# Four modulation groups change place: two from matmuls to multiply-and-sum in the mixer, two from the mixer into the feed-forward

## The chip, the cores and the metric

The kernel runs on one core of one Trainium2 chip. The metric is the time of one execution on the device in microseconds (us), lower is better. Engines are named TensorE (PE in the profile; its weight loads are PEld), VectorE (DVE), ScalarE (ACT), GpSimd (POOL) and SyncE (SP, which here only issues DMAs).

## The reference, cut to what matters

A two-layer encoder over two sequences of 256 and 512 tokens, 1024 wide, float32. Each layer is modulated by a conditioning vector c: a matrix product of silu(c) with a 1024 x 6144 matrix gives six vectors of 1024, for the shift, the scale and the gate of the layer's two halves.

```python
def trunk(x, c, adaln_w, adaln_b, norm_g, ...):
    for l in range(DEPTH):                       # 2 layers
        mod = jax.nn.silu(c) @ adaln_w[l] + adaln_b[l]
        sh1, sc1, g1, sh2, sc2, g2 = [t[:, None, :] for t in jnp.split(mod, 6, axis=-1)]
        h = rmsnorm(x, norm_g[l, 0]) * (1 + sc1) + sh1
        y = mlstm_mixer(h, ...) if l == 0 else swa_mixer(h, ...)
        x = x + g1 * y
        h = rmsnorm(x, norm_g[l, 1]) * (1 + sc2) + sh2
        x = x + g2 * conv_ffn(h, ...)
    return rmsnorm(x, final_g)

def conv_ffn(h, w_up, conv_w, conv_b, w_down):
    u = conv1d(h @ w_up, conv_w, width=3) + conv_b       # 2 * 2816 channels
    return (silu(u[..., :D_FF]) * u[..., D_FF:]) @ w_down
```

The six vectors are called modulation groups 0 to 5 here. Both sequences (c has two rows) go through the same trunk.

## The kernel before, in words

All 768 tokens are kept transposed, channels on the 128 partitions. Every float32 operand of a large product is split into a high part (`hi`, rounded by a ScalarE copy) and a low part (`lo`, a VectorE subtraction), and a product is three matmuls: hi x hi, hi x lo, lo x hi (`fp_copy_split`, lines 271 to 279; `mm`, line 268). A weight is loaded by SP into one of five `raw` slots of 512 KB (`raw`, line 282), split into one of three `whi`/`wlo` pairs, and its slot is free when the subtraction has read it. All operations of the split have the lines 275 and 276 in the profile, and all ordinary matmuls line 269.

Larger things live in six slots called `slab`, 12 KB a partition, which are handed out by order of allocation and come free when the last instruction on the old content is done. In a feed-forward they hold: x (two), `urows` (two, the second in use to the end), and of each part p `yrow` (the convolved rows) and `g` (the gated product, split).

The order of instructions on each engine is planned at build time from an estimate of costs (`schedule_with_timeline_sim=True`), earlier lines of the program before later ones where both are ready; stretches under `manual_schedule` keep the written order on the engines named. On the chip every engine runs its list in order and waits by semaphores.

The modulation. Layer 0's groups 0 and 1 come first (`adaln`). Its groups 2 to 5 are computed inside the mLSTM mixer on TensorE by `adaln_g`: eight loads of 512 KB of `adaln_w`, 32 matmuls of 256 columns against `silc` (silu(c), 32 columns wide, four side by side), two copies, two transposes and the sums with the bias. Layer 1's 48 columns of 128 (six groups of eight) are computed inside the same mixer on VectorE by `adaln_v`: of each column, 128 rows of the transposed matrix (`adaln_t`, 512 KB) are loaded into a `raw` slot, and for each sequence s one instruction multiplies them with silu(c), laid out along every partition (`row`), and sums along the row (`tensor_tensor_reduce`, line 538 in the profile, with the read of the sum behind it). A column is loaded one step before it is used.

Both are generators, and the mixer calls them step by step: `self.step(self.fill)` for the columns and `self.step(self.fillp)` for the matmul groups stand between its projections, its value tiles and its chunks, in heads 1 to 3; in the output gates behind the heads (line 892) only `fill` is stepped. What is left runs at the mixer's end (line 1742).

The feed-forward (`ffn`) has 11 parts of 256 gate and 256 value channels. Part p: `up(p)` computes two pairs of 128-channel rows with a seven-product scheme (`pair`; GpSimd makes the sums of weight quarters, lines 1383 to 1395; the matmuls have lines 1350, 1351 and 1353), convolves them (`conv`, lines 1587, 1589, 1590), applies silu (line 1597, held back into the next pair), multiplies on GpSimd and splits into `g` (`product`, lines 1602 and 1603). `down(p - 1)`, the product of the previous part with its share of `w_down`, comes behind `up(p)`, and adds its result to x with the gate (`resid`, line 602).

Of the kernel before, what the change touches and what calls it, by code (L numbers as in the profile page):

```python
# [11 lines left out]
F32 = mybir.dt.float32  # L12
R = mybir.dt.float32r
# [168 lines left out]
class Net:  # L182
# [335 lines left out]
                    self.cst(NG + (2 * l + i) * 8, 8), ALU.add, ALU.mult,  # L518
                )

    def adaln_v(self, l, pool):

        nc = self.nc
        stt = nc.vector.scalar_tensor_tensor
        row = pool.tile([P, 2, 1024], F32, name="crow")
        nc.sync.dma_start(row, self.crow.to_broadcast([P, 2, 1024]))
        junk = pool.tile([P, 1024], F32, name="junk")
        mod = self.mod[l]
        fetch = lambda j: self.raw(self.io["adaln_t"][j])
        nxt = fetch(0)  # L530
        yield
        for j in range(48):
            w, nxt = nxt, fetch(j + 1) if j < 47 else None
            with ExitStack() as order:
                if j == 0:
                    order.enter_context(self.tc.issue_after(self.opened.ins))
                for s in range(2):
                    nc.vector.tensor_tensor_reduce(  # L538
                        out=junk, in0=w, in1=row[:, s], scale=1.0, scalar=self.cst(AB + 48 * l + j),
                        op0=ALU.mult, op1=ALU.add, accum_out=mod[:, j, s : s + 1],  # L540
                    )
            i = {15: 0, 39: 1}.get(j)
            if i is not None:
                for s in range(2):
                    stt(
                        self.gain[l][i][:, :, s], mod[:, j - 7 : j + 1, s], 1.0,
                        self.cst(NG + (2 * l + i) * 8, 8), ALU.add, ALU.mult,
                    )
            yield
# [105 lines left out]
    def product(self, o, w, act, c0, c1, ks):  # L655
        wh, wl = (t.rearrange("p (k m) -> p k m", k=KC) for t in w)
        for k in ks:
            ah, al = act(k, c0, c1)
            self.mm(o, wh[:, k], ah, k == 0, False)
            self.mm(o, wh[:, k], al, False, False)  # L660
            self.mm(o, wl[:, k], ah, False, k == KC - 1)
# [910 lines left out]
    def ffn(self, l, xt, pool, last_tile, apply, keep=None):  # L1572
# [22 lines left out]
        def silu(yrow):  # L1595
            for j in range(2):
                nc.scalar.activation(yrow[:, j], yrow[:, j], AF.Silu)

        def product(yrow, g):
            for j in range(2):  # L1600
                y = yrow[:, 2 + j]
                nc.gpsimd.tensor_tensor(y, y, yrow[:, j], ALU.mult)  # L1602
                self.fp_copy_split(g[:, 0, j], g[:, 1, j], y)

        def up(p):
            urow = urows[0] if p == 0 else urows[1]
            fixed = lambda i: self.bank[i][:, :H]
            if p == 0:
                eng = mybir.EngineType
                self.ready(HALVES[0])  # L1610
                with self.tc.manual_schedule(engines={eng.PE, eng.Activation, eng.DVE}):
                    behind[:] = self.head(u0, last_tile, pool, urows, mark, early)
            yrow = self.slab([P, 4, TG])
            g = self.slab([P, 2, 2, TG], R)
            for i in range(2):
                if p:
                    rows = [urow[:, 2 * i + j] for j in range(2)]
                    with ExitStack() as order:
                        for ins in behind[2 * i :] if p == 1 else ():
                            order.enter_context(self.tc.issue_after(ins))  # L1620

                        other = p == i == 1
                        bank = lambda j: self.pa()[:, :H] if j == 1 and other else fixed(j)
                        self.pair(pool, u0 + 3 * p + i, bank, rows, p == 1, held.pop() if held else None)
                for j in range(2):
                    conv(urow[:, 2 * i + j], yrow[:, 2 * i + j], i * FC + 2 * p + j)
                if i == 0:
                    held.append(lambda: silu(yrow))
            if p:
                product(yrow, g)  # L1630
            else:
                gate = held.pop()
                held.append(lambda: (gate(), product(yrow, g)))
            return g

        def mark(t):

# [45 lines left out]

        prev = None
        for p in range(NPART):
            g = up(p)
            if prev is not None:
                down(*prev)
            prev = (p, g)
        down(*prev)  # L1690


# [27 lines left out]
    def first(self, pool):  # L1720
# [15 lines left out]
            self.nc.gpsimd.memset(t.bitcast(F32), 0.0)  # L1736
        hi, lo = (t.rearrange("p (j m) -> p j m", m=32)[:, :, 0:4] for t in gates)
        self.fp_copy_split(hi, lo, narrow.rearrange("p (j m) -> p j m", m=4))
        self.fillp = chain(*(self.adaln_g(0, grp) for grp in range(2, 6)))
        self.fill = self.adaln_v(1, pool)  # L1740
        act = self.mlstm(pool, gates, xt)
        for _ in chain(self.fillp, self.fill):
            pass
# [53 lines left out]
def _pack(inp):  # L1797
# [42 lines left out]
            w[u + 2] = _unit_D(inp["ffn_w_down"][l][p * 256 : (p + 1) * 256])  # L1840
    arr["w"] = w
    arr["adaln_w"] = np.ascontiguousarray(inp["adaln_w"][:1])
    arr["adaln_t"] = np.ascontiguousarray(inp["adaln_w"][1].T).reshape(48, P, D)
    arr["crow"] = np.ascontiguousarray(c.T.reshape(16, P))
    arr["rel_bias"] = np.ascontiguousarray(inp["rel_bias"])
    return arr
# [25 lines left out]
```

## Time and profile before

| what | value |
|---|---|
| time, median of 3 runs | 1808.51 us (1806.85 to 1808.69) |
| the profiled execution's own time | 1808.25 us, span 1806.4 us |
| granted TensorE clock, mean | 0.996 |
| busy: PE / PEld / DVE / ACT / POOL | 1773.1 / 1644.4 / 1384.8 / 887.8 / 488.2 us |
| HBM traffic | 176.77 MB read, 6.44 MB written, 101 GB/s over the span |

The stages lie, by the trace, so: the opening to about 65 us, the mLSTM mixer to about 425 us (its output gates from 353 us), its output projection and the first feed-forward to about 1000 us, the attention mixer, its projection and the second feed-forward to the end. Busy time of an engine counts its instructions' time on the engine alone; matmuls overlap, so that of PE is a union. A wait in the trace names the instruction that waited and the one that ended its wait.

### The profile page before, as it was taken

To read this page: it belongs to the slowest core of one execution; us is meant where nothing else is said; L and a number is where in the kernel's file an instruction comes from. 1 tells how busy PE (TensorE), PEld (TensorE's weight loads), DVE (VectorE), ACT (ScalarE), POOL (GpSimd) and SP (SyncE) were. 2 spreads that over 40 slices of the span, in tenths; PEclk is the share of its full clock that TensorE was granted. 3 is DMA by queue.
4 is the path that set the end of the run, shared out by engine and by line. 5 is a ranking of instruction groups with operands and counts; after the bars stand their busy time and mean duration, and the time that the engine had idled before them with its cause. 6 is when DMAs were issued, how large, how long until landed. Compare 5 with 4: busy or idle time off the path is not lost.

```text
span 1806.4 us, 28907 instructions
## 1 busy us (share of the span) xinstructions
PE 1773.1 (98%) x11206; PEld 1644.4 (91%) x11206; DVE 1384.8 (77%) x2219; ACT 887.8 (49%) x1789; POOL 488.2 (27%) x397
## 2 busy tenths in 40 slices
PE   7999999999999999999999999999999999999998
PEld 4988888889998999999999999889989999999997
DVE  4876777895799778777777867767998777777877
ACT  4544433444565444444444657665564444444443
POOL 3000000031024333333331313320144333333323
PEclk9999999999999999999999999999999999999999
DMA  9344665656212222222223331234122222222212
GB/s 360 98 140 135 196 207 180 215 180 219 71 59 71 62 67 71 70 71 71 67 64 94 106 93 42 60 92 138 48 82 71 71 71 71 70 70 71 70 36 71
DMA packets 64997, 185.08 MB, mean 102 GB/s; under 512 B 6247, under 2 KB 24839, under 8 KB 64732
## 3 DMA queue, kind: packets, MB, share of 16 engines
q1 hardware_dynamic: 64284, 182.72, 31.3%
q8 instruction: 88, 1.44, 0.3%
q10 hardware_dynamic: 576, 0.52, 0.1%
q14 instruction: 49, 0.40, 0.1%
HBM read 176.77 MB, written 6.44 MB: 101 GB/s over the span
## 4 chain that ended last, share of the span: by engine, by line
PE 87%; DVE 5%; DMA 3%; ACT 3%; issue 1%; POOL 1%; SPq 0%; DVEq 0%; ACTq 0%; POOLq 0%
PE ps L269 28%; PE pa L269 24%; PE ps L1350 11%; PE ps L1351 10%; PE ps L1353 10%; DMA raw<-in_adaln_t_dram 1%; PE pa L1189 1%; DVE junk L538 1%; DMA slab<-in_adaln_w_dram 1%; DVE wlo L276 1%; PE pa L1350 0%; PE pa L1351 0%; PE pa L1353 0%; ACT zh L1301 0%; DMA raw<-in_adaln_w_dram 0%
## 5 line engine op out<-in xcount | busy, mean ns | idle before, releaser
L275 ACT CAST whi<-raw 128x1024 fp32r<-128x1024 f32 (+1 forms) x231 | 241.0, 1045 | 339.0 <-PE pa L269 144.4
L276 DVE TENSOR_TENSOR wlo<-raw,whi 128x1024 fp32r<-128x1024 f32 (+1 forms) x231 | 312.6, 1354 | 119.1 <-ACT whi L275 116.8
L269 PE MATMUL pa<-slab,whi 128*128 128x256 f32 (+1 forms) x1280 | 307.6, 335 | 0.0
L269 PEld LDWEIGHTS pa<-slab,whi 128*128 128x128 f32 x1280 | 222.2, 188 | 21.6 <-DVE slab L602 0.4
L602 DVE SCALAR_TENSOR_TENSOR slab<-pa,mod,slab 128x256 f32<-128x256 f32 (+1 forms) x320 | 187.2, 603 | 62.7 <-PE pa L269 62.6
L269 PE MATMUL pa<-slab,wlo 128*128 128x512 f32 (+1 forms) x640 | 205.7, 334 | 0.0
L269 PE MATMUL ps<-zh,whi 128*128 128x256 f32 (+1 forms) x560 | 188.1, 337 | 0.3 <-ACT zh L948 0.3
L269 PE MATMUL ps<-zl,whi 128*128 128x256 f32 (+1 forms) x560 | 183.6, 330 | 0.5 <-DVE zl L563 0.5
L269 PE MATMUL ps<-zh,wlo 128*128 128x256 f32 (+1 forms) x560 | 181.7, 330 | 0.0
L1350 PE MATMUL ps<-zh,whi 128*128 128x384 f32 x504 | 172.6, 342 | 3.8 <-ACT nt L1421 2.0
L269 PE MATMUL ps<-slab,whi 128*128 128x384 f32 (+2 forms) x704 | 172.0, 329 | 0.9 <-DVE slab L276 0.5
L1351 PE MATMUL ps<-zl,whi 128*128 128x384 f32 x504 | 169.9, 337 | 0.8 <-DVE zl L1307 0.8
L1353 PE MATMUL ps<-zh,wlo 128*128 128x384 f32 x504 | 169.1, 336 | 0.0
L538 DVE CUSTOM_DVE_ANT_0 junk<-raw,crow,cstt 128x1024 f32<-128x1024 f32 x96 | 125.2, 1305 | 25.1 <-DMA raw<-in_adaln_t_dram 24.5
L1386 POOL TENSOR_TENSOR raw<-raw,raw 128x512 f32<-128x512 f32 x40 | 53.8, 1344 | 319.4 <-DVE wlo L276 246.3
L269 PEld LDWEIGHTS pa<-slab,wlo 128*128 128x128 f32 x640 | 120.4, 188 | 13.2 <-DVE wlo L276 0.4
L1602 POOL TENSOR_TENSOR slab<-slab 128x772 f32<-128x772 f32 x44 | 86.5, 1969 | 163.7 <-DVE slab L1590 150.5
L1589 DVE SCALAR_TENSOR_TENSOR slab<-slab,cstt,slab 128x771 f32<-128x771 f32 x88 | 105.4, 1200 | 26.5 <-ACT slab L1587 26.4
L269 PEld LDWEIGHTS ps<-slab,whi 128*128 128x128 f32 x704 | 122.5, 188 | 3.4 <-ACT whi L275 0.9
L269 PEld LDWEIGHTS ps<-zh,whi 128*128 128x128 f32 x560 | 106.8, 191 | 12.8 <-issue 3.5
L269 PEld LDWEIGHTS ps<-zl,whi 128*128 128x128 f32 x560 | 106.8, 191 | 9.5 <-DVE zl L563 0.7
L269 PE MATMUL ps<-slab,wlo 128*128 128x384 f32 (+2 forms) x352 | 114.8, 328 | 0.1
(301 smaller groups left out, 4286.8 us busy)
## 6 DMA issues: line engine op xcount, KB each, us to landing
raw<-in_w_dram SPq DMA_DIRECT2D x208, 512.0 KB, 3.7
raw<-in_adaln_t_dram SPq DMA_DIRECT2D x48, 512.0 KB, 4.2
raw<-in_adaln_w_dram SPq DMA_DIRECT2D x36, 512.0 KB, 4.5
slab<-in_x_dram SPq DMA_DIRECT2D x12, 512.0 KB, 7.2
slab<-in_adaln_w_dram SPq DMA_DIRECT2D x11, 512.0 KB, 9.2
slab<-mrows SPq DMA_DIRECT2D x8, 384.0 KB, 6.3
xs<-slab SPq DMA_DIRECT2D x6, 512.0 KB, 3.6
bt<-brow SPq DMA_DIRECT2D x16, 192.0 KB, 3.1
```

The source lines that it names most:

```text
L269: self.nc.tensor.matmul(out, lhsT, rhs, start=start, stop=stop)
L275: nc.scalar.copy(hi, src)
L276: return nc.vector.tensor_tensor(lo, src, hi.bitcast(F32), ALU.subtract)
L538: nc.vector.tensor_tensor_reduce(out=junk, in0=w, in1=row[:, s], scale=1.0, scalar=self.cst(AB + 48 * l + j), op0=ALU.mult, op1=ALU.add, a ...
L602: return self.nc.vector.scalar_tensor_tensor(x, o, self.mod[l][:, gc + c, q : q + 1], x, ALU.mult, ALU.add)
L1189: nc.tensor.transpose(pp[:, ks], b.t[:, e, ks], self.ident)
L1350: mm(o, wh[:, k], hi[k], start=start and k == 0, stop=False, skip_group_check=True)
L1351: mm(o, wh[:, k], lo[k], start=False, stop=False, skip_group_check=True)
L1353: mm(o, wl[:, k], hi[k], start=False, stop=k == 3, skip_group_check=True)
L1386: tt(q[0], q[2], q[0], ALU.subtract)
L1589: stt(y[:, 1:], u[:, :-1], w(0), y[:, 1:], ALU.mult, ALU.add)
L1602: nc.gpsimd.tensor_tensor(y, y, yrow[:, j], ALU.mult)
```

## The change

Layer 0's groups 4 and 5 are no longer computed by `adaln_g`; `fillp` holds groups 2 and 3 alone. `adaln_v` becomes `by_rows(columns, room)`, which takes any list of columns of both layers (0 to 47 layer 0, 48 to 95 layer 1) and the room for `row` and its scratch. In the mixer it runs over layer 1's groups 0 and 1 (48 to 63), layer 0's groups 4 and 5 (32 to 47) and layer 1's groups 2 and 3 (64 to 79): 48 columns, as before. Layer 1's groups 4 and 5 (80 to 95) run inside the first layer's feed-forward: at part 2 a third slab is taken for `row` (1 MB) and scratch, and each pair (two to a part) from part 2 on makes one step. To free that slab `g` is allocated later: `product` now only multiplies, and the splits (`parted`) with their allocation of `g` come behind `down(p - 1)` in parts 1 to 10, in both layers. The transposed matrix in memory holds both layers.

```diff
--- before.py
+++ after.py
@@ -518,21 +518,21 @@
                     self.cst(NG + (2 * l + i) * 8, 8), ALU.add, ALU.mult,
                 )
 
-    def adaln_v(self, l, pool):
+    def by_rows(self, columns, room):
 
         nc = self.nc
         stt = nc.vector.scalar_tensor_tensor
-        row = pool.tile([P, 2, 1024], F32, name="crow")
+        row, junk = room[:, :2], room[:, 2]
         nc.sync.dma_start(row, self.crow.to_broadcast([P, 2, 1024]))
-        junk = pool.tile([P, 1024], F32, name="junk")
-        mod = self.mod[l]
-        fetch = lambda j: self.raw(self.io["adaln_t"][j])
+        fetch = lambda i: self.raw(self.io["adaln_t"][columns[i]])
         nxt = fetch(0)
         yield
-        for j in range(48):
-            w, nxt = nxt, fetch(j + 1) if j < 47 else None
+        for i, at in enumerate(columns):
+            w, nxt = nxt, fetch(i + 1) if i + 1 < len(columns) else None
+            l, j = divmod(at, 48)
+            mod = self.mod[l]
             with ExitStack() as order:
-                if j == 0:
+                if i == 0:
                     order.enter_context(self.tc.issue_after(self.opened.ins))
                 for s in range(2):
                     nc.vector.tensor_tensor_reduce(
@@ -1596,11 +1596,15 @@
             for j in range(2):
                 nc.scalar.activation(yrow[:, j], yrow[:, j], AF.Silu)
 
-        def product(yrow, g):
+        def product(yrow):
             for j in range(2):
                 y = yrow[:, 2 + j]
                 nc.gpsimd.tensor_tensor(y, y, yrow[:, j], ALU.mult)
-                self.fp_copy_split(g[:, 0, j], g[:, 1, j], y)
+
+        def parted(yrow, g):
+            for j in range(2):
+                self.fp_copy_split(g[:, 0, j], g[:, 1, j], yrow[:, 2 + j])
+            return g
 
         def up(p):
             urow = urows[0] if p == 0 else urows[1]
@@ -1611,7 +1615,9 @@
                 with self.tc.manual_schedule(engines={eng.PE, eng.Activation, eng.DVE}):
                     behind[:] = self.head(u0, last_tile, pool, urows, mark, early)
             yrow = self.slab([P, 4, TG])
-            g = self.slab([P, 2, 2, TG], R)
+            if p == 2 and l == 0:
+                self.fill = self.by_rows(range(80, 96), self.slab([P, 3, 1024]))
+                self.step(self.fill)
             for i in range(2):
                 if p:
                     rows = [urow[:, 2 * i + j] for j in range(2)]
@@ -1626,12 +1632,15 @@
                     conv(urow[:, 2 * i + j], yrow[:, 2 * i + j], i * FC + 2 * p + j)
                 if i == 0:
                     held.append(lambda: silu(yrow))
+                if p > 1:
+                    self.step(self.fill)
             if p:
-                product(yrow, g)
-            else:
-                gate = held.pop()
-                held.append(lambda: (gate(), product(yrow, g)))
-            return g
+                product(yrow)
+                return lambda: parted(yrow, self.slab([P, 2, 2, TG], R))
+            g = self.slab([P, 2, 2, TG], R)
+            gate = held.pop()
+            held.append(lambda: (gate(), product(yrow), parted(yrow, g)))
+            return lambda: g
 
         def mark(t):
 
@@ -1683,10 +1692,10 @@
 
         prev = None
         for p in range(NPART):
-            g = up(p)
+            part = up(p)
             if prev is not None:
                 down(*prev)
-            prev = (p, g)
+            prev = p, part()
         down(*prev)
 
 
@@ -1736,8 +1745,8 @@
             self.nc.gpsimd.memset(t.bitcast(F32), 0.0)
         hi, lo = (t.rearrange("p (j m) -> p j m", m=32)[:, :, 0:4] for t in gates)
         self.fp_copy_split(hi, lo, narrow.rearrange("p (j m) -> p j m", m=4))
-        self.fillp = chain(*(self.adaln_g(0, grp) for grp in range(2, 6)))
-        self.fill = self.adaln_v(1, pool)
+        self.fillp = chain(*(self.adaln_g(0, grp) for grp in range(2, 4)))
+        self.fill = self.by_rows([*range(48, 64), *range(32, 48), *range(64, 80)], pool.tile([P, 3, 1024], F32, name="crow"))
         act = self.mlstm(pool, gates, xt)
         for _ in chain(self.fillp, self.fill):
             pass
@@ -1840,7 +1849,7 @@
             w[u + 2] = _unit_D(inp["ffn_w_down"][l][p * 256 : (p + 1) * 256])
     arr["w"] = w
     arr["adaln_w"] = np.ascontiguousarray(inp["adaln_w"][:1])
-    arr["adaln_t"] = np.ascontiguousarray(inp["adaln_w"][1].T).reshape(48, P, D)
+    arr["adaln_t"] = np.ascontiguousarray(inp["adaln_w"].transpose(0, 2, 1)).reshape(96, P, D)
     arr["crow"] = np.ascontiguousarray(c.T.reshape(16, P))
     arr["rel_bias"] = np.ascontiguousarray(inp["rel_bias"])
     return arr
```

## The prediction

> **What bounds the kernel now.** I read the page's first and fourth parts, then the waits of TensorE by stage, then the stages' windows.
>
> ```profile
> PE 1773.1 (98%) x11206; PEld 1644.4 (91%) x11206; DVE 1384.8 (77%) x2219; ACT 887.8 (49%) x1789; POOL 488.2 (27%) x397
> PE 87%; DVE 5%; DMA 3%; ACT 3%; issue 1%; POOL 1%; SPq 0%; DVEq 0%; ACTq 0%; POOLq 0%
> ```
>
> TensorE is busy nearly throughout and carries the chain that ended last; the reader should still ask whether that holds in the two stages that change. The waits of TensorE, first for 130 to 430 us (the mixer), then for 600 to 980 us (the first layer's feed-forward), answer it with one line each:
>
> ```profile
> PE pa L738 <- ACT slab L734: 0.4, 1, 0.4
> PE ps L1350 <- ACT ps L1410: 0.2, 1, 0.2
> ```
>
> So in both stages TensorE waits for practically nothing: its issued work is the time there. The windows of four stretches (columns: busy time of PE, its weight loads, DVE, ACT, POOL; granted clock; DMA share; GB/s) tell how near the others are:
>
> ```profile
> 260.00:310.00 50.00, 49.63 (x340) 41.01 (x339) 32.01 (x70) 16.57 (x48) 3.64 (x2) 1.00 0.59 198
> 310.00:353.00 43.00, 43.00 (x324) 36.27 (x323) 33.79 (x72) 17.04 (x40) 0.00 (x0) 1.00 0.63 205
> 353.00:420.00 67.00, 67.00 (x407) 60.02 (x406) 59.45 (x96) 29.73 (x64) 23.51 (x16) 1.00 0.63 202
> 700.00:800.00 100.00, 100.00 (x569) 94.23 (x568) 77.34 (x87) 46.07 (x73) 39.84 (x24) 1.00 0.22 68
> ```
>
> The clock is 1.00 in all four, so it plays no part. VectorE is next: 71% of 260 to 353 us, 89% of 353 to 420 us, 77% in the feed-forward.
>
> **The change part by part.**
>
> *Two groups leave TensorE.* Modulation groups 4 and 5 of layer 0 are no longer matmuls against silc. The matmuls that read silc, all four groups, in the mixer's first and second half, and the transposes that end a group:
>
> ```profile
> L269 PE MATMUL ps<-raw,silc 128*32 128x256 f32 x256 | 22.0, 386 | 0.0
> 130.00:195.00 65.00, 5.96 (x80) 2.19 (x80) 0.00 (x0) 0.00 (x0) 1.00 0.46 148
> 195.00:260.00 65.00, 3.83 (x48) 1.37 (x48) 0.00 (x0) 0.00 (x0) 1.00 0.58 190
> 260.00:353.00 93.00, 12.24 (x128) 4.05 (x128) 0.00 (x0) 0.00 (x0) 1.00 0.61 201
> L507 PE MATMUL ps<-kct,sb x8: 271/272/273, 190.5 to 352.6; 128*128 128x128 f32 x8
> ```
>
> A group has 64 records. The first two groups took 5.96 + 3.83 = 9.8 us, the last two, which go, 12.2 us; the last two are cut into smaller bursts, and each burst's last matmul overlaps what follows it. Half of all four is 11.0 us, and I take that; ends 9.8 and 12.2. Four transposes of 0.27 us go too; they overlap their neighbours, and I count 0.3 us. Gain on TensorE 11.3 us.
>
> *What those bursts covered.* Some stand directly before work that was only just ready. TensorE's timeline at the end of head 3:
>
> ```profile
> 342.02 0.63 PE L269 MATMUL ps<-raw,silc 128*32 128x256 f32 x6
> 342.58 2.17 PE L269 MATMUL pa<-slab,PT 128*128 128x258 f32 x16
> 344.69 0.63 PE L269 MATMUL ps<-raw,silc 128*32 128x256 f32 x4
> 345.25 1.46 PE L269 MATMUL pa<-slab,PT 128*128 128x258 f32 x10
> 346.63 1.06 PE L269 MATMUL ps<-raw,silc 128*32 128x256 f32 x12
> 347.62 0.74 PE L269 MATMUL pa<-slab,PT 128*128 128x258 f32 x4
> ```
>
> From start to start the six cost 342.58 - 342.02 = 0.56 us and the twelve 0.99 us: they do hold TensorE's queue. If the PT products were not ready earlier, TensorE would idle there instead. The one wait of the mixer, 0.4 us for L734, stands behind such a burst. The order of the matmuls is planned anew at each build and the next head's projections are independent, so most of this refills. I charge 1.3 us (the 0.4 us grown by one burst of 0.9 to 1.0); ends 0 and 5.6, half the gain.
>
> *The mixer's column work on VectorE keeps its count.* 48 columns before, 48 after (16, 16 and 16), at the same steps, in the same room; only their order and source differ. Two groups' copies and sums leave VectorE (some 1 us). SP issues 16 fewer loads of adaln_w there. Where a load now is late, VectorE waits at a column:
>
> ```profile
> L538 DVE CUSTOM_DVE_ANT_0 junk<-raw,crow,cstt 128x1024 f32<-128x1024 f32 x96 | 125.2, 1305 | 25.1 <-DMA raw<-in_adaln_t_dram 24.5
> L538 DVE DVE_READ_ACCUMULATOR2_ANT mod<- 128x1 f32 x96 | 7.8, 81 | 0.0
> ```
>
> With fewer loads competing for the five raw slots that wait can only shrink; I count nothing. With 11.3 us less of TensorE, VectorE's share of 260 to 353 us goes from 65.8 of 93 to about 65 of 82 (79%), below the 89% of the next stretch, where TensorE never waited.
>
> *Sixteen columns enter the first layer's feed-forward.* Parts 2 to 9 get two columns each: 2 x 2 x (1.305 + 0.081) = 5.5 us of VectorE per part. A part's length is the distance between two first products on GpSimd:
>
> ```profile
> 700.59 1.87 POOL L1602 TENSOR_TENSOR slab<-slab 128x772 f32<-128x772 f32 x1 [5.40 <-DVE slab L1590]
> 747.04 1.87 POOL L1602 TENSOR_TENSOR slab<-slab 128x772 f32<-128x772 f32 x1 [5.40 <-DVE slab L1590]
> ```
>
> That is 46.45 us. VectorE's 77% of it is 35.9 us, with the columns 41.4 us or 89%. That is the share of 353 to 420 us, where 26 column instructions, POOL work at 35% and a full TensorE lived side by side. This row is the nearest and it says: no cost. But GpSimd slows VectorE:
>
> ```profile
> 740.35 1.29 POOL L1383 TENSOR_TENSOR raw<-raw 128x512 f32<-128x512 f32 x1 [7.23 <-DMA raw<-in_w_dram]
> 740.45 2.27 DVE L276 TENSOR_TENSOR wlo<-raw,whi 128x1024 fp32r<-128x1024 f32 x1 [2.06 <-ACT whi L275]
> 743.58 1.21 DVE L276 TENSOR_TENSOR wlo<-raw,whi 128x1024 fp32r<-128x1024 f32 x1
> ```
>
> The same split took 1.21 us alone and 2.27 us when it began just after a GpSimd sum. The Trainium skill ("SBUF — State Buffer", section "Who interferes with whom") gives a rule for it: a VectorE instruction with two SBUF inputs and a GpSimd one that reads SBUF exclude each other for a whole instruction, in order of issue. The pair above agrees, 1.06 us lost to a sum with 1.19 us left. By the rule, with POOL at 40%, about 13 of the 32 instructions would be held by up to a sum's length, at 1.06 us each some 14 us more on VectorE, 93% of a part rather than 89%. On TensorE that costs only what is not covered. I charge 1.5 us for all parts; ends 0 and 32 x 1.06 = 34 us.
>
> *The loads.* Sixteen loads and the 1 MB broadcast row join SP's queue of weight loads, which always waits for a slot. What SP waited for over the span, what GpSimd waited for in the feed-forward, and the load:
>
> ```profile
> SPq L284 <- DVE wlo L276: 1098.6, 167, 20.6
> POOL raw L1386 <- DVE wlo L276: 121.8, 16, 14.2
> POOL raw L1383 <- DMA raw<-in_w_dram: 66.6, 15, 8.8
> raw<-in_adaln_t_dram SPq DMA_DIRECT2D x48, 512.0 KB, 4.2
> ```
>
> A column holds a slot for its landing (4.2 us) and its two instructions (2.7 us), 6.9 us, or 13.8 us a part of the 5 x 46.45 = 232 us of slots: weight loads come 13.8 / 5 = 2.8 us later. The next user, the sums of L1383, precedes L1386, and L1386 stands idle 121.8 / 16 = 7.6 us waiting for a split, not for the load: 2.8 us is hidden. The row is fetched once, in part 2, into a slab that is free only when part 1's splits are done; queued behind it on SP are part 2's weights, and the first column. A part is 46 us; I count nothing.
>
> *The splits of g move behind the down-projection before them.* In layer 0 with the extra slab two slabs are left for yrow and g, so g(p) waits for the last matmul of part p-1's down-projection, and the next yrow for those splits:
>
> ```profile
> L276 DVE TENSOR_TENSOR slab<-slab,slab 128x772 fp32r<-128x772 f32 x44 | 53.1, 1208 | 0.0
> L275 ACT CAST slab<-slab 128x772 fp32r<-128x772 f32 x44 | 36.8, 836 | 26.6 <-POOL slab L1602 26.2
> 721.88 0.49 DVE L602 SCALAR_TENSOR_TENSOR slab<-pa,mod,slab 128x256 f32<-128x256 f32 x1 [0.92 <-PE pa L269]
> 726.65 1.04 ACT L1587 ACTIVATE slab<-slab,cstt 128x772 f32<-128x772 f32 x1 [1.88 <-DVE slab L1423]
> ```
>
> Two casts and two subtractions, 0.84 + 2 x 1.21 = 3.3 us in a pipeline, fit between that part's last residual (721.9 us) and the next part's first convolution (726.7 us); behind other splits on VectorE they may run 2 us late, but their reader is the next down-projection, over 20 us on. The last part of each layer has no next up-projection between: its splits stand behind at most the sixteen residuals, two subtractions at 1.21 us, 2.4 us a layer if they came last. They are ready in the middle of that down-projection and go when ready: 0; end 4.8.
>
> **Sum.** -11.0 - 0.3 + 1.3 + 1.5 = -8.5 us on TensorE's path. The profiled execution took 1808.25 us (span 1806.4), 0.26 below the runs' median of 1808.51, so the two can be used alike. 1808.25 - 8.5 = 1799.75, say 1799.8 us.
>
> **The rivals.**
>
> *The cover is lost.* The bursts filled waits, and half of their time stays as idle before L738, L720 and the PT products. For it: the 0.4 us at L734. Against: the stretch without bursts, 353 to 420 us, has none. 1808.25 - 5.65 + 1.5 = 1804.1 us. [...]
>
> *VectorE comes late in the feed-forward (slower).* A column stands before a split or an eviction that TensorE needs. For it: in both feed-forwards one such wait exists, in part 1:
>
> ```profile
> PE ps L1353 <- DVE s1l L276: 2.8, 2, 1.4
> ```
>
> At 1.4 us for each of 16 steps it is 22.4 us: 1808.25 - 11.3 + 1.3 + 22.4 = 1820.7. It decides from (10.0 + 3.6) / 8 = 1.7 us a part. Against: that row is two waits in 1806 us, and 353 to 420 us has 89% without any.
>
> *The slots bind.* If the 2.8 us of later weights showed in each of 8 parts: 22.4 us, the same time, told apart by who is waited for (ACT whi behind DMA). Half hidden, it gives 1809.5, no change. Against: L1386's idle time.
>
> **How the numbers follow.** About 0.2% (3.6 us) is what a measurement tells from no change. My forecast with its own range, 1796 to 1803: 0.62, all faster. The cover lost: 0.18, of it 0.12 faster, 0.06 same, as it ends at the border. VectorE late: 0.13, of it 0.08 slower, 0.05 same where it is partial. Slots: 0.07, of it 0.01 faster, 0.03 same, 0.03 slower. Faster 0.75, same 0.14, slower 0.11. The range goes from 1796 (11.3 + 1.2 for the longer bursts, no cost) to 1807, which leaves out the worse half of the last three cases.
>
> **What would show it.** Right: 128 silc matmuls instead of 256 in the mixer, TensorE full from 260 us on, the out-projection starting some 10 us earlier; 32 column instructions in parts 2 to 9 of the first feed-forward, 1.3 to 2.3 us long; a part still 46.4 to 46.7 us. Wrong: parts 2 to 9 above 48 us, with TensorE waiting for DVE s1l, wlo or L1423; TensorE waiting for ACT L734 or the PT casts after 260 us; new waits at the layers' last down-projection.

## The result, and the profile after

The changed kernel takes 1815.53 us (median of six runs, 1812.78 to 1817.0) beside 1808.06 us for the kernel before on the same chip (six runs, 1806.8 to 1808.78): a ratio of 1.0040, 95% interval 1.0027 to 1.0053. It is slower by 7.5 us; 1799.8 was predicted, in a range of 1796 to 1807. Times here and below are medians of fast runs; one slow run, 5135.94 us of the last kernel in the table, is left out.

The page of the changed kernel, first and fourth part: TensorE has shed 6.6 us of busy time, VectorE has taken on 40.9 us, and the chain leans on VectorE more than before (7% instead of 5%).

```profile
PE 1766.5 (97%) x11074; PEld 1642.4 (91%) x11074; DVE 1425.7 (79%) x2277; ACT 889.0 (49%) x1787; POOL 488.1 (27%) x397
PE 82%; DVE 7%; DMA 4%; issue 3%; ACT 2%; POOL 2%; SPq 0%; DVEq 0%; POOLq 0%; ACTq 0%
```

First products on GpSimd mark the parts. Of the kernel before: parts 0, 2 and 8.

```profile
539.18 2.51 POOL L1602 TENSOR_TENSOR slab<-slab 128x772 f32<-128x772 f32 x1 [5.97 <-ACT slab L1597]
607.37 1.86 POOL L1602 TENSOR_TENSOR slab<-slab 128x772 f32<-128x772 f32 x1 [6.79 <-DVE slab L1590]
885.80 1.89 POOL L1602 TENSOR_TENSOR slab<-slab 128x772 f32<-128x772 f32 x1 [3.92 <-DVE slab L1590]
```

The same three of the changed kernel:

```profile
522.81 2.51 POOL L1602 TENSOR_TENSOR slab<-slab 128x772 f32<-128x772 f32 x1 [5.97 <-ACT slab L1597]
606.21 1.85 POOL L1602 TENSOR_TENSOR slab<-slab 128x772 f32<-128x772 f32 x1 [5.10 <-DVE slab L1590]
893.69 1.86 POOL L1602 TENSOR_TENSOR slab<-slab 128x772 f32<-128x772 f32 x1 [0.96 <-DVE slab L1590]
```

The mixer gained 539.18 - 522.81 = 16.4 us. From part 0 to 2 the lead shrinks to 1.2 us: 83.4 us instead of 68.2, a loss of 15.2. From part 2 to 8 another 9.1 goes: 287.5 instead of 278.4, 1.5 a part. The marks are GpSimd's, and TensorE's work between them is not quite the same, as the windows from part 0 to 2 show, of before and of the change:

```profile
539.18:607.37 68.19, 65.12 (x366) 61.18 (x365) 59.58 (x61) 36.60 (x57) 27.43 (x15) 1.00 0.26 81
522.81:606.21 83.40, 73.62 (x389) 68.27 (x388) 71.65 (x80) 38.97 (x61) 29.71 (x15) 0.96 0.35 108
```

The change has 23 matmuls more there and 18 fewer from part 2 to 8 (1569 instead of 1587). At 278.43 / 1587 = 0.175 us each, some 4 us of the 15.2 are work that has moved ahead of the mark and some 3 us must be added to the 9.1: as losses they are rather 11 and 12 us. After the last columns nothing more is lost, and the second layer's feed-forward, with the later splits alone, keeps its parts of some 46.4 us.

What TensorE waited for from 525 to 1010 us (in total, times, longest), the five largest of the change; before, the largest there was 1.4 us for `s1l`:

```profile
PE ps L1353 <- DVE wlo L276: 4.9, 7, 1.2
PE ps L1350 <- ACT ps L1399: 4.8, 1, 4.8
PE pa L269 <- DVE slab L602: 2.9, 5, 1.5
PE ps L1350 <- ACT whi L275: 2.5, 5, 0.5
PE ps L1350 <- ACT ps L1410: 2.2, 1, 2.2
```

The 4.8 us is in part 1 to 2, and VectorE's timeline there tells where it begins. The row's transfer was issued at 568.87 us; the first column stands in VectorE's list behind five residuals, waits for the row, and behind it stands the split `wlo`:

```profile
568.72 2.31 DVE L602 SCALAR_TENSOR_TENSOR slab<-pa,mod,slab 128x512 f32<-128x512 f32 x5
575.83 1.28 DVE L538 CUSTOM_DVE_ANT_0 slab<-raw,slab,cstt 128x1024 f32<-128x1024 f32 x1 [4.80 <-DMA slab<-crows]
577.04 0.08 DVE L538 DVE_READ_ACCUMULATOR2_ANT mod<- 128x1 f32 x1
577.04 1.22 DVE L276 TENSOR_TENSOR wlo<-raw,whi 128x1024 fp32r<-128x1024 f32 x1
```

From that split the chain of releases runs over three sums on GpSimd (to 584.8 us), then a cast, a step of the convolution and a copy on ScalarE (L275, L1587, L1399), to TensorE. Its timeline: the wait, and then matmuls that start 0.32 us apart instead of 0.17, at a granted clock of 0.64 from 587.2 to 592 us.

```profile
581.89 0.34 PE L1351 MATMUL ps<-zl,s1h 128*128 128x384 f32 x1
582.06 0.34 PE L1353 MATMUL ps<-zh,s1l 128*128 128x384 f32 x1
587.21 0.69 PE L1350 MATMUL ps<-zh,whi 128*128 128x384 f32 x1 [4.81 <-ACT ps L1399]
587.70 0.52 PE L1351 MATMUL ps<-zl,whi 128*128 128x384 f32 x1
588.02 0.52 PE L1353 MATMUL ps<-zh,wlo 128*128 128x384 f32 x1
```

In parts 3 to 8 the loss has another shape. At the end of each down-projection stand two short waits, here in part 3:

```profile
675.13 0.28 PE L269 MATMUL pa<-slab,wlo 128*128 128x256 f32 x1
675.24 0.33 PE L1350 MATMUL ps<-zh,whi 128*128 128x384 f32 x1
675.41 0.34 PE L1351 MATMUL ps<-zl,whi 128*128 128x384 f32 x1
675.59 0.33 PE L1353 MATMUL ps<-zh,wlo 128*128 128x384 f32 x1
676.43 0.44 PE L1350 MATMUL ps<-yh,whi 128*128 128x384 f32 x1 [0.50 <-ACT whi L275]
676.71 0.34 PE L1351 MATMUL ps<-yl,whi 128*128 128x384 f32 x1
677.68 0.45 PE L1353 MATMUL ps<-yh,wlo 128*128 128x384 f32 x1 [0.64 <-DVE wlo L276]
```

The cast waits for the last matmul of the down-projection; only then can this weight be cast and split, and TensorE's list holds three matmuls to cover that:

```profile
675.33 1.05 ACT L275 CAST whi<-raw 128x1024 fp32r<-128x1024 f32 x1 [8.49 <-PE pa L269]
```

The two waits are 1.14 us; the rest of the 1.5 is slower starts behind them and single waits for L602. No column holds that split up: the last one on VectorE ended some 12 us before. In the kernel with the mixer's part alone (below) the same place looks so:

```profile
706.53 0.28 PE L269 MATMUL pa<-slab,wlo 128*128 128x256 f32 x1
706.73 1.05 ACT L275 CAST whi<-raw 128x1024 fp32r<-128x1024 f32 x1 [8.42 <-PE pa L269]
707.17 0.34 PE L1350 MATMUL ps<-yh,whi 128*128 128x384 f32 x1
```

There the first `yh` matmul starts at 707.17 us, before the cast ends at 707.78, so on a weight that was split earlier, and TensorE does not wait. In the change that weight is not split ahead.

### The profile page after: what moved, and what is told of

It reads as the page before. It is cut to its first block, busy times and chain, and to the rows that moved or that the text cites. A ratio compares the mean times of both kernels' runs of the same rounds, so it can differ in the third digit from the quotient of the medians.

```text
span 1814.2 us, 28734 instructions
## 1 busy us (share of the span) xinstructions
PE 1766.5 (97%) x11074; PEld 1642.4 (91%) x11074; DVE 1425.7 (79%) x2277; ACT 889.0 (49%) x1787; POOL 488.1 (27%) x397
## 4 chain that ended last, share of the span: by engine, by line
PE 82%; DVE 7%; DMA 4%; issue 3%; ACT 2%; POOL 2%; SPq 0%; DVEq 0%; POOLq 0%; ACTq 0%
PE ps L269 28%; PE pa L269 23%; PE ps L1350 9%; PE ps L1353 9%; PE ps L1351 9%; DVE wlo L276 2%; PE pa L1189 1%; DMA raw<-in_adaln_t_dram 1%; DMA slab<-in_adaln_w_dram 1%; DMA raw<-in_w_dram 1%; ACT whi L275 1%; DVE crow L538 1%; DVE slab L1589 1%; PE pa L1350 0%; PE pa L1351 0%
## 5 line engine op out<-in xcount | busy, mean ns | idle before, releaser
L275 ACT CAST whi<-raw 128x1024 fp32r<-128x1024 f32 (+1 forms) x231 | 241.2, 1045 | 343.4 <-PE pa L269 141.4
L602 DVE SCALAR_TENSOR_TENSOR slab<-pa,mod,slab 128x256 f32<-128x256 f32 (+1 forms) x320 | 185.8, 602 | 46.2 <-PE pa L269 46.1
L1350 PE MATMUL ps<-zh,whi 128*128 128x384 f32 x504 | 172.5, 342 | 10.0 <-ACT ps L1399 5.5
L538 DVE CUSTOM_DVE_ANT_0 crow<-raw,crow,cstt 128x1024 f32<-128x1024 f32 x96 | 124.1, 1293 | 18.5 <-DMA raw<-in_adaln_t_dram 17.9
L1383 POOL TENSOR_TENSOR raw<-raw 128x512 f32<-128x512 f32 x40 | 62.6, 1566 | 260.5 <-DMA raw<-in_w_dram 225.4
L1386 POOL TENSOR_TENSOR raw<-raw,raw 128x512 f32<-128x512 f32 x40 | 63.9, 1598 | 250.9 <-DVE wlo L276 180.8
L269 PEld LDWEIGHTS ps<-zh,whi 128*128 128x128 f32 x560 | 106.5, 190 | 12.2 <-issue 3.1
```

Source lines behind the costliest of these rows:

```text
L269: self.nc.tensor.matmul(out, lhsT, rhs, start=start, stop=stop)
L275: nc.scalar.copy(hi, src)
L538: nc.vector.tensor_tensor_reduce(out=junk, in0=w, in1=row[:, s], scale=1.0, scalar=self.cst(AB + 48 * l + j), op0=ALU.mult, op1=ALU.add, a ...
L602: return self.nc.vector.scalar_tensor_tensor(x, o, self.mod[l][:, gc + c, q : q + 1], x, ALU.mult, ALU.add)
L1350: mm(o, wh[:, k], hi[k], start=start and k == 0, stop=False, skip_group_check=True)
L1383: tt(q[2], q[2], q[3], ALU.add)
```

## The experiments

All are edits of the changed kernel; the diffs are cut to the lines that matter. The table has, of each profile, the first product of part 0, the time from there to part 2, and the lengths of the later parts that have columns (of all later parts, where none has). The names are explained under it.

| kernel | ratio to before, 95% interval | part 0 at | 0 to 2 | later parts, us |
|---|---|---|---|---|
| before | 1 | 539.2 | 68.2 | 46.0 to 46.7 |
| the change | 1.0040 (1.0027 to 1.0053) | 522.8 | 83.4 | 47.7 to 48.2 |
| mixer only | 0.9917 (0.9902 to 0.9932) | 524.2 | 68.2 | 46.1 to 46.7 |
| slab and row held | 0.9951 (0.9936 to 0.9965) | 522.0 | 76.4 | 45.9 to 46.7 |
| columns, no loads | 1.0048 (1.0032 to 1.0065) | 522.4 | 86.5 | 51.1, 49.5 |
| late first column | 1.0026 (1.0017 to 1.0036) | 524.3 | 76.3 | 47.6 to 48.1 |
| early row | 1.0031 (1.0019 to 1.0043) | 522.5 | 83.8 | 45.6 to 48.4 |
| early row, late first | 0.9982 (0.9973 to 0.9992) | 523.5 | 71.5 | 47.6 to 48.0 |
| tiny columns | 0.9975 (0.9965 to 0.9984) | 523.5 | 73.7 | 46.8 to 47.3 |
| paced, no loads | 1.0014 (1.0004 to 1.0024) | 523.4 | 69.9 | 47.5 to 50.1 |
| behind down | 1.0005 (0.9995 to 1.0014) | 522.0 | 76.4 | 46.6 to 48.7 |
| one a part | 1.0152 (1.0137 to 1.0167) | 550.3 | 75.9 | 47.9 to 48.8 |
| halves | 1.0070 (1.0055 to 1.0085) | 522.6 | 74.7 | 48.4 to 50.8 |
| four a part | 1.0060 (1.0045 to 1.0075) | 523.3 | 75.5 | 56.9, 52.6, 50.0 |
| ahead of pair | 1.0030 (1.0018 to 1.0041) | 521.3 | 80.4 | 47.2 to 48.8 |
| before down | 0.9941 (0.9925 to 0.9958) | 524.6 | 69.4 | 46.4 to 47.9 |
| place alone | 0.9989 (0.9980 to 0.9999) | 523.0 | 78.1 | 46.2 to 47.7 |
| 64 in the mixer, left over | 1.0038 (1.0023 to 1.0053) | 546.2 | 68.2 | 46.0 to 46.9 |
| 64 in the mixer, shared | 1.0063 (1.0044 to 1.0082) | 547.9 | 68.2 | 46.2 to 46.7 |

### The halves of the change

Mixer only:

```diff
-            if p == 2 and l == 0:
-                self.fill = self.by_rows(range(80, 96), self.slab([P, 3, 1024]))
-                self.step(self.fill)
```

> The changed kernel without its feed-forward part: layer 1's groups 4 and 5 are not computed (their columns are zeros), no slab and no row in the feed-forward; the mixer part and the later splits stay. All theories: the mixer's gain alone, 16 us by the trace of the changed kernel (its first product of the feed-forward starts at 522.8 instead of 539.2 us), so 1792 us, and parts of 46.4 us in both feed-forwards. If the later splits cost something by their place in the program alone, more than that: 1795 or above.

1793.29 us. The mixer's part is worth 14 to 15 us by itself, and the later splits of `g` cost nothing: no part is longer than before.

Slab and row held, with no loads and two column instructions at the end (`hold` fetches the row as `by_rows` does):

```diff
+                self.fill = self.hold(self.slab([P, 3, 1024]), 16, False)
```

> As the run before, but the slab is taken and the row loaded at part 2 and both are kept to part 9, with no loads of columns and one column instruction pair at the end. Theory SLOTS (column loads sit in raw slots before the row is there, and take slots from weights) and theory VECTOR (the column instructions delay what TensorE waits for): 1792 to 1793 us. Theory SLAB (with two slabs for yrow and g the splits stand behind the down-projection and the next part starts late): some 1.2 us in each of parts 3 to 8, so 1800 us.

1798.98 us. Only part 1 to 2 is longer, by 8.2 us; a missing slab in every part is refuted. The two instructions need nothing but the row, the planner put them into part 1, and VectorE waits there as in the change, with `wlo` behind:

```profile
571.79 1.29 DVE L559 CUSTOM_DVE_ANT_0 slab<-slab,cstt 128x1024 f32<-128x1024 f32 x1 [4.62 <-DMA slab<-crows]
573.00 0.08 DVE L559 DVE_READ_ACCUMULATOR2_ANT mod<- 128x1 f32 x1
573.00 0.48 DVE L615 SCALAR_TENSOR_TENSOR slab<-pa,mod,slab 128x256 f32<-128x256 f32 x1
573.40 1.22 DVE L276 TENSOR_TENSOR wlo<-raw,whi 128x1024 fp32r<-128x1024 f32 x1
```

So one instruction at the wrong place in VectorE's list costs 8.2 us: VectorE's wait of 4.6 ends in one of TensorE of 3.96, and behind that matmuls start 0.32 us apart for 5.9 us (a clock of 0.72 granted from 578 to 590 us). That was not among the theories; it is the first cause.

Columns without loads, multiplying the row with itself:

```diff
+                self.fill = self.hold(self.slab([P, 3, 1024]), 16, True)
```

> As the run before, with all 32 column instructions, which multiply the two halves of the row with each other, so that nothing is loaded into raw slots for them. SLOTS: 1793 us, as without them. VECTOR: most of the feed-forward's loss of 24 us comes back, 1807 us or above. SLAB: 1800 us.

1816.82 us. With no load to wait for, the columns ran bunched in parts 2 to 4, so it shows only that VectorE's instructions can cost as much as the change loses without any load in a slot.

### The row and the first loads

Late first column: loads and columns start one part later (`wait` is 2), the row as in the change.

```diff
+        for _ in range(wait):
+            yield
         nxt = fetch(0)
```

> The whole computation; the row is loaded in part 2 as in the changed kernel, but the first column's load comes one part later, columns in parts 3 to 10. SLOTS: part 2's loss of 15 us goes (no slot is held while the row is awaited), parts 3 to 8 keep their 1.2 us each: 1800 us. VECTOR and SLAB: no or little gain over the changed kernel, 1812 to 1815 us.

1812.08 us: part 0 to 2 falls by 7.1 us, and 8.1 stay. VectorE still waits 4.8 us for the row. Each of the parts with columns is as long as in the change.

Early row: slab and row at the end of `up(1)` instead of at part 2, the first column as in the change.

```diff
             if p:
                 product(yrow)
+                if p == 1 and l == 0:
+                    self.fill = self.by_rows(range(80, 96), self.slab([P, 3, 1024]))
+                    self.step(self.fill)
```

> The whole computation. The third slab is taken and the row fetched at the end of part 1's up-projection, where part 0's yrow is long done, instead of at part 2; columns at their old steps. FETCH (the row's transfer waits on SP for part 1's splits and part 2's weights stand behind it, and the first columns' loads hold raw slots meanwhile): part 1 to 2 and part 2 to 3 fall to 46.5 to 48.5 us, and only some 1.4 us in each of 8 parts stay over the kernel with the mixer's part alone (1793.3): about 1804, range 1801 to 1807. SHORTAGE (it is having one slab less at part 2, whenever the row comes): part 1 to 2 stays above 42 us at no gain there, and the time is 1812 as with the later first load.

1813.16 us. The expected gain did not come: the first column moved forward with the row, VectorE again waited for it (3.8 us), and the loss spread over two parts. This points at the nearness of the row's first reader to its transfer, wherever the row stands in SP's queue. Both edits together test it:

> The whole computation. The late first column (parts 3 to 10) with one more edit: slab and row at the end of part 1's up-projection instead of at part 2's start. With the early row alone part 0 to 2 took 83.8 us where the mixer's part alone takes 68.2, and VectorE waited 3.8 us for the row's transfer with a column at the head of its list. LATE ROW (in both kernels the loss at parts 1 and 2 is a column, or weights, waiting behind the row): now the row lands two parts ahead of its first reader and no column load is near, part 0 to 2 falls to 68 to 70 us, time 1803 to 1806. SHORTAGE (one slab less at parts 1 and 2 delays yrow or g themselves): part 0 to 2 stays at 76 us or more, time 1811 to 1814.

1805.14 us. VectorE waits for the row nowhere, part 0 to 2 is 71.5 us, and 3.3 us of the 15.2 are left (2 of them ten matmuls more between the marks). By the times, 1.0040 to 0.9982, the two edits give back 10.5 us.

### The time of the columns or their place

Tiny columns: the early row, all loads, each instruction on 8 of 1024 elements.

```diff
-                        out=junk, in0=w, in1=row[:, s], scale=1.0, ...
+                        out=junk[:, :n], in0=w[:, :n], in1=row[:, s, :n], scale=1.0, ...
```

> As the early row, with all 16 loads and all 32 column instructions, but each reads 8 of its 1024 elements (so the modulation groups 4 and 5 of layer 1 are not the full sums). VECTOR (the columns' VectorE time delays splits): parts 3 to 9 at 46.3 to 46.8 us, time 1793 to 1796. SLOTS (the loads take raw slots and room in SP's queue, and weights come later): parts stay at 47.9, time about 1804 as with the full columns.

1802.94 us: parts of 46.8 to 47.3. The loads, with columns this short, cost some 0.6 us a part (281.9 instead of 278.3 us from part 2 to 8).

Paced, no loads: the early row, no load, full columns behind the last convolution of their step.

```diff
+                if after:
+                    order.enter_context(self.tc.issue_after(after.pop().ins))
```

> As the early row, without the 16 loads: each column instruction multiplies the row with itself at full length, and is held behind the last convolution instruction of its step, so that columns stay two to a part (layer 1's groups 4 and 5 are not computed). VECTOR: parts at 47.9 us, time about 1804. SLOTS: parts at 46.3 to 46.8, time 1793 to 1796. If both were needed together, this and the tiny columns would both lie near 1794.

1810.44 us, parts of 47.5 to 50.1: without any load the parts are longer than in the change. So VectorE's instructions cost without any load in a slot, though TensorE waits here at another line (the copy that is L1410 in the change). Is it their time or their place? In the next kernels the columns stand elsewhere. Behind down (with the early row):

```diff
-                if p > 1:
-                    self.step(self.fill)
...
                 down(*prev)
+            if p > 1:
+                self.step(self.fill, 2)
```

> As the early row, but both columns of a part stand in the program behind the down-projection, later than all splits and convolutions of the part, so that the planner puts them behind that work. ORDER (columns cost because they stand ahead of a split of wlo or whi that TensorE needs): parts come down from 47.9 towards 46.6 us, time 1794 to 1799. AMOUNT (5.5 us more of VectorE in a part cost 1.4 wherever they stand): parts 47.9, time about 1804.

1808.12 us. Parts between 46.6 and 48.7: undecided.

One a part: eight columns in the feed-forward, one to a part, and 56 in the mixer.

> The whole computation. Eight of the 16 columns go back into the mixer (56 there; steps of the matmul groups that are left over drive columns), eight stay, one to a part in parts 3 to 10, with the early row. If VectorE's time in a part costs in proportion: parts at 47.1 us (half of the 1.2 to 1.4 over 46.5). If it costs only past a threshold near 85% of a part: parts at 46.4 to 46.8. If any column in a part costs the same, 47.7. The mixer's eight columns more are 22 us of VectorE over 325 us: hidden, or, if VectorE is already the bound between 260 and 340 us (94% there), up to 11 us later. Time 1795 to 1805.

1835.37 us. In the mixer the eight columns more cost 27 us (part 0 at 550.3). In the feed-forward half the columns cost no less: parts of 47.9 to 48.8. The cost is not in proportion to VectorE's time; but VectorE waits 16.4 us for these columns' loads, 8.3 in the change, so that late loads may be part of it.

The next four start from the early row with the late first column. Halves of columns at four places, two of them inside the down-projection:

> The whole computation, as the early row with the late first column, but a step is half a column (one instruction and its read), and there are four places to a part: behind each pair's convolutions and ahead of each half of the down-projection. PLACE (a 2.8 us block of VectorE ahead of a split that TensorE is due to read is what costs): blocks of half the length, parts 46.5 to 47.1, time 1796 to 1801. AMOUNT: parts 47.6 to 47.8 as before, time 1805.

1819.95 us, parts of 48.4 to 50.8: shorter blocks at more places are worse. Here columns do stand ahead of the split at the end of the down-projection: two halves start at 668.24 and 669.57 us, the first after 1.30 us of waiting for its load, and `wlo` follows at 671.96.

Four a part, in parts 3 to 6:

```diff
-                    self.step(self.fill)
+                    self.step(self.fill, 1 if p == 2 else 2)
```

> The whole computation, as the early row with the late first column, but four columns a part in parts 3 to 6 and none in parts 7 to 10. AMOUNT: a part with 11 us of columns has 47 us of VectorE in 46.5 of TensorE, so 49 to 50, the sum over four parts 11 us or more, time 1804 to 1810. PLACE (a part with any column loses one wait of 1.2 us): four parts at 47.8, time 1799 to 1801.

1818.42 us, the time of neither theory. From part 2 to 6 it is 204.9 us, some 19 over four parts of 46.5. VectorE was busy 90, 86 and 93% of the three longest parts, so it was not full; TensorE waited 13.4 us for residuals on VectorE (L604). Amount and place are not told apart here.

Ahead of the pair, `self.step(self.fill)` at the top of the loop over i:

> The whole computation, as the early row with the late first column, but each column stands in the program ahead of its pair instead of behind the pair's convolutions. AMOUNT: parts 47.6 to 47.8, time 1805. PLACE: another length of part, anywhere from 46.5 to 49, and TensorE waits for another line than wlo and whi at the end of the down-projection.

1813.37 us, parts of 47.2 to 48.8, and TensorE now waits for DVE L604 (L602 in the change; the edit shifts the lines by two), 14 times.

Before down, two steps between `up(p)` and `down(p - 1)`:

```diff
             part = up(p)
+            if p > 1:
+                self.step(self.fill, 2)
             if prev is not None:
                 down(*prev)
```

> The whole computation, as the early row with the late first column, but both columns of a part stand between its up-projection and the down-projection of the part before. AMOUNT: parts 47.6 to 47.8, time 1805. PLACE: another length of part, anywhere from 46.5 to 49, and TensorE waits at another place; of the four, one at or below 46.8 would settle it.

1797.32 us, 0.9941 (0.9925 to 0.9958): the same 16 columns, two to a part, in parts of 46.4 to 46.8 but for two. The next comparison is of VectorE's share. The window 640 to 740 us (busy PE, PEld, DVE, ACT, POOL; clock; DMA share; GB/s) of the change:

```profile
640.00:740.00 100.00, 97.59 (x554) 91.83 (x553) 86.29 (x102) 45.88 (x73) 33.82 (x20) 1.00 0.29 90
```

of the columns before down:

```profile
640.00:740.00 100.00, 99.54 (x567) 94.15 (x566) 86.38 (x104) 46.17 (x73) 38.97 (x23) 1.00 0.28 89
```

of one column a part:

```profile
640.00:740.00 100.00, 97.16 (x546) 89.90 (x545) 80.28 (x91) 43.00 (x68) 30.84 (x20) 1.00 0.24 77
```

and of the mixer only:

```profile
640.00:740.00 100.00, 100.00 (x574) 94.59 (x573) 79.12 (x88) 44.69 (x71) 40.49 (x24) 1.00 0.20 64
```

VectorE is as busy in the second as in the first, 86.4 and 86.3%, and TensorE idles 0.5 instead of 2.4%. At 80% (third) TensorE idles 2.8%. So up to two columns a part VectorE's share does not decide; the place in the program does. How the place reaches TensorE can be read at the end of a down-projection of this kernel (TensorE; L1352 is L1350 of the change):

```profile
663.45 0.28 PE L269 MATMUL pa<-slab,wlo 128*128 128x256 f32 x1
663.57 0.34 PE L1352 MATMUL ps<-zh,whi 128*128 128x384 f32 x1
...
667.58 0.34 PE L1355 MATMUL ps<-bq,wlo 128*128 128x384 f32 x1
667.75 0.34 PE L1352 MATMUL ps<-yh,whi 128*128 128x384 f32 x1
```

and the cast and the split meanwhile:

```profile
663.65 1.05 ACT L275 CAST whi<-raw 128x1024 fp32r<-128x1024 f32 x1 [1.55 <-PE pa L269]
664.74 1.23 DVE L276 TENSOR_TENSOR wlo<-raw,whi 128x1024 fp32r<-128x1024 f32 x1 [0.48 <-ACT whi L275]
```

The cast waits for the last matmul of the down-projection here too; but from 663.57 to 667.75 TensorE's list has 24 matmuls on weights that are ready, 4.2 us, where the change has three, 0.5 us. The planner orders all engines together, and where a column stands in the program changes TensorE's list as well. The three matmuls and the two waits stand in the late first column, the early row, both together and the halves too. So "place" means all that the planner makes of it: no run moved the columns with TensorE's list held as it was.

Place alone: the change with only the two steps moved before down.

> The whole computation: the change with one edit, both columns of a part between its up-projection and the down-projection before; row and first load at part 2's start, as in the change. ADDITIVE (row and loads cost 12 to 14 us in parts 1 to 3, the place 1.3 us a part after them, apart from each other): parts 4 to 9 at 46.4 to 46.8 us, part 1 to 3 as long as in the change (49.1 and 47.7) or a few us less, time 1803 to 1808. ROW WAS PLACE TOO (the loss at part 2 came from where the first columns stand): parts 1 to 3 come down to 36 and 46.6, time 1796 to 1799.

1805.60 us. Later parts are as short as hoped but for two of 47.7 and 47.6; part 0 to 2 is 78.1 us, with VectorE's wait for the row again 4.5 us. The two causes nearly add: as ratios, row and first loads are worth 0.58% at the old place and 0.48% at the new one, the place 0.51% and 0.41%.

### All columns in the mixer

The list of the mixer with all 64 columns, none in the feed-forward: once with the steps as they are (the last 16 behind the mixer), once with the unused steps of the matmul groups driving columns too.

> The whole computation. No column in the feed-forward; the mixer's list has all 64 columns (layer 1's groups 4 and 5 at its end) and the steps are unchanged, so the last 16 are left over and run behind the mixer, beside the output projection. They are 44 us of VectorE. HIDDEN (VectorE is at 58 to 65% from 340 to 455 us): the first product of the feed-forward stays at 522 to 525 us, time 1793 to 1796. BOUND (they collide with what the output projection needs from VectorE): the first product 5 to 20 us later, 1798 to 1812.

> As 64 columns left over, but the steps that the two groups taken off TensorE no longer use drive columns too, so that all 64 stand between the mixer's matmuls from head 2 on. HIDDEN: time 1793 to 1797. BOUND (VectorE is at 94% from 260 to 340 us already): TensorE waits for VectorE in heads 2 and 3, the first product 5 to 20 us later, 1798 to 1812.

1815.27 and 1817.89 us. Both begin the feed-forward 22 to 24 us late. In the first, ScalarE's cast `whi` waits for a weight load (first line, 360 to 430 us), and TensorE for that cast (second line, 100 to 525 us):

```profile
ACT whi L275 <- DMA raw<-in_w_dram: 16.9, 3, 14.2
PE ps L269 <- ACT whi L275: 19.2, 2, 18.2
```

So the weight loads behind more column loads bind in the mixer, not VectorE, as far as these lines go; no run separated the two there.

## Why the prediction was wrong

**Two groups leave TensorE: right in kind, too small.** Predicted 11.3 less 1.3 for lost cover; by the first product of part 0 the change gained 16.4, and the table's other kernels with 48 columns in the mixer 14.6 to 17.9. Part of that spread lies in the opening: the first burst of matmuls on `silc` starts at 130.4 to 134.3 us in these kernels and at 133.9 before, though no edit touches what stands ahead of it. From that burst on, the change gained 14.9 us: 11.7 are the bursts of groups 4 and 5, from start to start in the records, 0.2 the four transposes, 3.0 other matmuls that stand closer together. So the bursts were worth nearly the upper end (12.2), not the half, and the charge of 1.3 has the wrong sign; TensorE waits for nothing from 130 to 430 us. Why the other matmuls stand closer no run isolated. The Trainium skill ("Perfetto Trace Analysis", section "Identifying the Most-Contended Engine") uses the share of weight loads to judge how close TensorE is to roofline, its limit. It is not a measure of what removed matmuls return: these had 4.05 us of weight loads and held TensorE for 11.7.

**The row "fetched once" at "nothing": the step that failed.** It looked at SP's queue and at a part of 46 us. What counted is VectorE's list: the first reader of the row had its turn 2.2 us after the transfer's issue, VectorE waited 4.8 us for it to land, and the split behind it held GpSimd's sums and then TensorE. With the first columns' loads at the same place it made 15.2 us between the marks, about 11 as a loss; moving both gave back 10.5.

**Sixteen columns, 1.5 us: mis-sized, with the right argument for amount.** They cost 9.1 us from part 2 to 8 by the marks, about 12 with the matmuls that had moved ahead. That 89% of VectorE need not cost TensorE anything holds (86.4% beside 99.5%); that therefore it does not, doesn't follow. The rival named the sign, TensorE waiting for `wlo`, and put it at 0.13; its mechanism, a column ahead of a split, is that of part 1 to 2 and of the halves, while in the change's later parts VectorE itself waits for the cast, which TensorE's list covers too little. At 1.5 us a part the rival would have stayed below its own point of 1.7, but with the row's loss the sum passed it. With one of the two misses mended the time is 1805.14 us (row and first loads moved) or 1805.60 us (columns before down), faster than before and inside the range; it is their sum that turned the sign. That the mixer gave some 5 us more than forecast hid as much of it: luck.

**The port rule: near the estimate.** By the Trainium skill ("SBUF — State Buffer", section "Who interferes with whom") a VectorE instruction with two SBUF inputs contends with a GpSimd one that reads SBUF. The prediction's estimate from that was 13 of the 32 instructions held and some 14 us more on VectorE. The 32 instructions (shortest, median, longest), and their sum and mean:

```profile
L538 DVE CUSTOM_DVE_ANT_0 slab<-raw,slab,cstt x32: 1271/1284/2776, 575.8 to 887.1; 128x1024 f32<-128x1024 f32 x32
L538 DVE CUSTOM_DVE_ANT_0 slab<-raw,slab,cstt 128x1024 f32<-128x1024 f32 x32 | 50.0, 1562 | 13.1 <-DMA raw<-in_adaln_t_dram 8.3 <-DMA slab<-crows 4.8
```

Ten of them took over 1.32 us, up to 2.78, and each of the ten began while GpSimd was at work. At the median all 32 would be 41.1 us, so the holds cost 8.9. The trace agrees with the rule; the cost came out a third below the estimate. VectorE's busy total rose by 40.9 us only, as it counts neighbours that overlap once.

**The loads, "hidden": nearly.** With tiny columns some 0.6 us a part; as the main cost in the feed-forward the slots are refuted. **The later splits, 0: right**, in both layers.

The sum by the marks of the two profiles: -16.4 + 15.2 + 9.1 - 0.7 (parts 8 to 10) + 0.6 (all behind) = 7.8 us, the difference of the spans, 1814.2 and 1806.4.

## What to carry to other kernels

An instruction that is put into an engine's list to use idle time costs by what stands behind it: ask of the first one whether its data has landed when its turn comes, and fetch a part earlier, with the first use later still. A share of busy time says whether the work can fit, not whether it does: after each move look at the wait of the bound engine, look at what the planner did to that engine's list, and try another place in the program before giving the work up. Here the same work at four places, with row and loads alike, gave 1797 to 1820 us.

## What the runs showed of the hardware

After a wait of 4.81 us matmuls started 0.32 us apart, for about 3 us; after 3.96 us, in the kernel with slab and row held, for 5.9. There the wait of 3.96 us and some 17 starts that come 0.15 us later each are 6.5 of the 8.2 us. The Trainium skill ("TensorE: Matmul & The Clock Gate", section "What's actually happening") gives half the clock after an idle window of some 3.4 us, which these waits agree with. A single idle wait of that length is not needed: in the change the clock also fell to 0.57 from 536 to 540 us, where TensorE had waited only 0.91 and 1.07 us, though it had been busy just 0.61 of the 2 us before:

```profile
534.00:536.00 2.00, 0.61 (x2) 0.30 (x2) 1.45 (x1) 2.00 (x3) 1.65 (x1) 1.00 0.35 137
536.00:540.00 4.00, 3.75 (x12) 3.67 (x13) 4.00 (x6) 3.63 (x7) 0.00 (x0) 0.57 0.20 35
```
